# A hybrid attention step on one core: the prompt heads' finish as a job of its own, with a block scratch, and cached loads tied to products

## The chip, the cores and the metric

The kernel runs on one core of a Trainium2 chip. The metric is the device time of one execution in microseconds (us). A core has five engines that run side by side, each through its own list of instructions in order: TensorE (PE, matrix products; PEld is its weight load), VectorE (DVE), ScalarE (ACT), GpSimd (POOL) and SyncE (SP). SP, ACT and POOL also issue DMA transfers; their queues are written SPq, ACTq and POOLq. An instruction that waits holds up all that stand behind it on its engine.

## What is computed

One step of a one-layer streaming encoder: 1024 prompt frames of one stream, and 16 new frames (samples) of each of 8 running streams with 1024 cached frames. Cut to what matters (batch and head reshapes left out):

```python
def reference(x_prompt, x_sample, cache_sb_k, cache_sb_v, state_ret, norm_pre, w_in, sb_head_norm, ret_head_norm, w_out, norm_post):
    # for the prompts, and again for the samples
    h = rms_norm(x, norm_pre)                                 # x: frames x 2048
    q_sb, k_sb, v_sb, gate_sb, q_r, k_r, v_r, gate_r = split(h @ w_in, 8)   # each 8 heads x 128
    q_r, k_r = rope(q_r), rope(k_r) * 128 ** -0.5
    # stick-breaking attention, strictly causal; samples also see the cached keys and values
    z = q_sb @ k_sb.T * 128 ** -0.5
    log_keep = where(strict, log_sigmoid(-z), 0)
    later = reverse_cumsum(log_keep) - log_keep               # over the keys
    o_sb = where(strict, exp(log_sigmoid(z) + later), 0) @ v_sb
    # retention: decayed scores inside a chunk of 64, plus the state carried from chunk to chunk
    o_r, state = retention(q_r, k_r, v_r, log_gamma)
    y = concat(head_rms_norm(o_sb, sb_head_norm) * silu(gate_sb), head_rms_norm(o_r, ret_head_norm) * silu(gate_r))
    return x + rms_norm(y @ w_out, norm_post)                 # and the new k_sb, v_sb, state
```

## The kernel before, in words

All data is float32. Each product of two float32 operands is made as three matmuls of high and low parts (`split` makes them: ACT the high part, DVE the low part; `wh`/`wl` for weights, `mh`/`ml` for the moving rows).

After RMSNorm and transposes the frames are worked in two groups. The first holds prompt tiles 0 to 3 and the sample tile (128 frames each), the second prompt tiles 4 to 7. In each group a loop of `i` from 0 to 7 goes over the heads. "Head 1.2" below is `i` = 2 of the second group (the code counts groups from 0). A head's projections stand in this order: retention q (`q_r`), `k_r`, at even `i` the value rows of two heads (`rows_vr`, `project_rows`), the retention gate, then the stick-breaking q, k, at even `i` the value rows of two heads, and the gate (`gate_sb`). In the second group a projection has 48 matmuls 512 wide, value rows 192 matmuls 256 wide. Samples ride along at even `i` in both groups (`decode`).

The attention work is not written in line. It consists of generators wrapped in `Job`: `tick()`, called after each product, moves on the one job that is due, and a `yield D_...` says how many products later it wants to go on. The constants D_* hold a pair where the two groups differ. `drain(job)` runs a job to its end at once. `place(inst)` binds an instruction behind the last product in the order only: no wait is added. A scheduler with its own costs then sets the final order of each engine.

The names and places that matter:
- `Out.finish`: the head norm of an attention row. DVE scales `so` (prompts, 128x512) by the inverse root mean square; ACTq writes it to a DRAM scratch `s_o` (`turn_out`); `D_TO` products later SPq reads it back in four transfers, turned by blocks (`turn_in`); `D_TI` products later DVE transposes it within blocks into a scratch `oT`, multiplies it with the gain and the gate `sg`, and ACTq writes `s_y`. The retention rows do the same with `ro` and `rg`; the samples' rows with `os` and `gs` (128x128).
- For the prompts' rows that scratch was `kT` (`finish(0, h, rest["sg"], kT, ...)`, line 844). `kT` is the tile into which ACT evacuates the key projection of the next head (line 892), and it has one buffer. On ACT `kh`, the high part of the keys, stands right behind it (L135).
- `sb_job` holds scores, `turn_out`/`turn_in` of the weights, the product with the values (`pa<-vn,kp`, line 588, after the transposition `kp<-be`, line 553) and the finish. The loop drains it after the next head's `q_sb` projection.
- The scores `z<-kh,qh` (own keys) and `z<-kph,qh` (the first group's keys) are line 564.
- `decode` reads cached keys (`kc`, four POOLq transfers each, line 616, three buffers) and cached values (`vc`, SPq, line 654, a pool of three shared with `kcT`); DVE transposes `kc` to `kcT` (line 646), PE multiplies with `vc` in `pd` (line 688).
- The projections have two PSUM banks for each half (`acc0`, `acc1`). A bank comes free once its evacuation is done; that of `gate_sb` goes into `sg`, a tile with one buffer that the head before still holds until its finish has written `s_y`.

After the second group comes the output projection: panels `a3<-wh3,mh` (lines 974 to 976), the first of which also carries the rest of head 1.7's jobs. That stretch, from the end of head 1.7's `gate_sb` to the last drained job, is called the tail below.

Of the kernel before, what the change touches and what calls it, by code (L numbers as in the profile page):

```python
# [36 lines left out]
D_ZP = (2, 2)  # L37
D_AV = (22, 20)
D_ZC = 24
# [5 lines left out]
V_BUFS = 3  # L45
D_RET = (9, 5)
D_TO = (26, 23)
# [11 lines left out]
def tile_hybrid_step(  # L59
# [231 lines left out]
    with ExitStack() as s1:  # L291
# [218 lines left out]
        def acc_tile():  # L510
            return psa.tile([P, 512], F32, name="pa", tag="pa")

        class Out:
# [9 lines left out]
            def finish(self, b, h, gT, oT, dst):  # L523
                rs = inv_rms(op, self.ssq, P, "o")
                nc.vector.tensor_tensor(
                    self.o, self.o, rs.unsqueeze(2).to_broadcast([P, self.nt, P]), ALU.mult
                )
                s = turn_out(self.o, f"s_o{b}_{h}_{self.nt}")
                yield D_TO[phase[0]]
                flat = self.o.rearrange("p k d -> p (k d)")  # L530
                turn_in(s, flat, nc.sync)
                yield D_TI[phase[0]]
                n = self.nt * P
                place(nc.vector.transpose(oT[:, :n], flat))
                nc.vector.scalar_tensor_tensor(
                    gT[:, :n], oT[:, :n], gains[:, b, h : h + 1], gT[:, :n], ALU.mult, ALU.mult
                )
                nc.scalar.dma_start(dst, gT[:, : self.nt * P])

        def z_pieces(n):  # L540
            return [(s, min(512, n - s)) for s in range(0, n, 512)]

        def stick_breaking(tiles, h, out, q2, keys, rest):
            todo = list(enumerate(tiles))
            lag, kinds = 2, ("pcr" if todo[0][1] else ("kp", "be", "cp"))
            rows = []
            for step in range(len(todo) + lag):
# [28 lines left out]
                if step >= lag:  # L576
# [4 lines left out]
                    if step >= len(todo):  # L581
                        yield D_TR[phase[0]]
                    while "vn" not in rest:
                        yield 3
                    vn = rest["vn"]
                    po = acc_tile()
                    for j in range(t + 1):
# [4 lines left out]
                    out.done(i)  # L592
                yield D_AV[phase[0]]

        def decode(h, qs, rest):
# [16 lines left out]
            def load(m):  # L612
                s, j, c = chunk(m)
                kc = dp.tile([P, 512], F32, name="kc", tag="kc", bufs=3)
                for i in range(4):
                    nc.gpsimd.dma_start(  # L616
                        kc[32 * i : 32 * i + 32, :].rearrange("p (k d) -> p k d", d=32),
                        cache_k[0, 2 * c + j, s * 512 : (s + 1) * 512, h, 32 * i : 32 * i + 32].rearrange(
                            "(k p) d -> p k d", p=32
                        ),  # L620
                    )
                return kc
# [28 lines left out]
            def load_v():  # L651
                k = len(values)
                vc = dp.tile([P, NB, P], F32, name="vc", tag="kv", bufs=V_BUFS)
                nc.sync.dma_start(
                    vc, cache_v[0, :, k * P : (k + 1) * P, h, :].rearrange("b p d -> p b d")
                )
                values.append(vc)
# [39 lines left out]
            out.done(0)  # L697
            oT = op.tile([P, P], F32, name="osT", tag="osT", bufs=1)
            ends.append(Job(out.finish(0, h, rest["gs"], oT, s_ys[h]), 2))

# [94 lines left out]
        def ret_branch(gi, g, h, rq, rk, rv, rg):  # L795
# [4 lines left out]
            s = turn_out(rk[:, : nt * P].rearrange("p (k t) -> p k t", t=P), f"s_rk{gi}_{h}")  # L800
            yield D_TO[phase[0]]
            raw = out.o.rearrange("p k d -> p (k d)")
            turn_in(s, raw, nc.sync)
            yield D_TI[phase[0]]
            place(nc.vector.transpose(rkn.rearrange("p k d -> p (k d)")[:, : nt * P], raw))
# [6 lines left out]

        def sb_branch(gi, tiles, h, out, q2, keys, kT, rest, ks):
            off = 4 * gi
# [18 lines left out]
            yield D_NAT[phase[0]]  # L833
            yield from stick_breaking(tiles, h, out, q2, keys, rest)
            vn = rest["vn"]
# [6 lines left out]
            while "sg" not in rest:  # L842
                yield 3
            yield from out.finish(0, h, rest["sg"], kT, s_y[gi][h][:, : 4 * P])

        from_h = lambda k: [(0, NMAX, s_h[:, k, :])]
        from_y = lambda k: [(0, 3 * P, s_y[0][k][:, : 3 * P])]
        ret_job = sb_job = dec_job = loads = None
        ends = []
        for gi, g in enumerate(GROUPS):  # L850
# [7 lines left out]
            for i in range(H):  # L858
# [21 lines left out]
                if sample:  # L880
                    drain(dec_job)
                    while len(ends) > 1:
                        drain(ends.pop(0))
                    qs = kq.tile([P, P], F32, name="qs", tag="qs")
                    nc.scalar.activation(qs, acc[1][0][:, 2 * P : 3 * P], AF.Copy)
                    dec_job = Job(decode(h, qs, rest), D_DEC)
                out = Out(4, "so")
                acc = project(pieces, mov, col(1, h))
# [11 lines left out]
                if gi == 1:  # L900
# [4 lines left out]
                    keys = [old, k2]  # L905
                sb_job = Job(sb_branch(gi, tiles, h, out, q2, keys, kT, rest, ks), D_NAT[phase[0]])
                if i % 2 == 0:
# [16 lines left out]
                if i == H - 1:  # L924
# [3 lines left out]
                    next(loads)  # L928
                acc = project(pieces, mov, col(3, h), loads, (2, 3))
                sg = ep.tile([P, NB_TOK], F32, name="sg", tag="sg")  # L930
                for a, (o, m) in acc:
# [55 lines left out]
        drain(dec_job)  # L987
        for job in ends:
            drain(job)
# [169 lines left out]
```

## Time and profile before

| | |
|---|---|
| median of 3 runs | 2593.51 us (2589.94 to 2596.11) |
| the profiled execution | 2584.93 us, of which the span in the trace is 2583.2 us |
| PE busy | 2398.9 us (93% of the span) |
| DVE busy | 1263.0 us (49%) |
| ACT busy | 932.9 us (36%) |
| POOL busy | 710.3 us (27%) |
| mean granted clock of TensorE | 0.961 of full speed |

PE is the busiest engine by far. So the time is PE's work, at the clock that it is granted, plus the stretches in which PE waits; those are what the order of the other engines' work can move. A row such as `PE z L564 <- ACT kh L135: 60.5, 4, 18.0` in the list of waits says: PE, at line 564, writing tile `z`, waited for ACT's write of `kh` at line 135; 60.5 us in all, 4 times, 18.0 us at the longest. In a timeline the columns are start and duration in us, engine, line and instruction; in brackets stands how long the engine had been idle, and what ended it.

### The profile page before, as it was taken

The page shows a single profiled execution, that of the slowest core. Times are in us where ns is not written, and L with a number is a line of the kernel's source. Part 1 is how long each engine was busy: PE and PEld are TensorE (multiplying, and loading weights), DVE is VectorE, ACT ScalarE, POOL GpSimd, SP SyncE. Part 2 cuts the span into 40 slices and gives each one's busy share as a digit, 9 for nine tenths or more (in the row PEclk, how much of TensorE's full clock was granted, in tenths as well). Part 3 has the DMA queues.
Part 4 walks back from the last instruction along what each step waited for, and adds up shares of the span by engine and source line. Part 5 has one row for each costly group of instructions (what it writes and reads, how often), then busy time and mean ns, then how long its engine had stood idle before and what let it go on. Part 6 is the DMA issues. An engine that isn't in the chain of part 4 may idle for free. (4 is left out here: it accounts for less than half of the span.)

```text
span 2583.2 us, 40506 instructions
## 1 busy us (share of the span) xinstructions
PE 2398.9 (93%) x14832; PEld 2113.2 (82%) x14832; DVE 1263.0 (49%) x2454; ACT 932.9 (36%) x1953; POOL 710.3 (27%) x1133
## 2 busy tenths in 40 slices
PE   7999999999999999899969996999799957999998
PEld 7999899979998998599748975897579745778787
DVE  7245534544455344555544554455544544465544
ACT  6333333323333333343333333333333342344343
POOL 3134214421442144214331433133313322000000
PEclk9999999999999999999989998999899978999999
DMA  7757846684658466866776667666766567576554
GB/s 240 183 131 159 209 106 158 139 205 104 159 138 206 107 162 142 216 170 160 149 149 158 162 147 150 161 159 145 161 157 160 136 165 172 182 225 198 172 177 146
DMA packets 635288, 421.30 MB, mean 163 GB/s; under 512 B 187856, under 2 KB 578000, under 8 KB 632656
## 3 DMA queue, kind: packets, MB, share of 16 engines
q1 hardware_dynamic: 526000, 287.30, 44.3%
q0 software_dynamic: 36608, 80.80, 13.9%
q10 hardware_dynamic: 72480, 50.61, 6.5%
q8 instruction: 116, 1.90, 0.3%
q14 instruction: 84, 0.69, 0.1%
HBM read 337.55 MB, written 81.00 MB: 162 GB/s over the span
## 5 line engine op out<-in xcount | busy, mean ns | idle before, releaser
L136 DVE TENSOR_TENSOR wl<-wr,wh 128x512 fp32r<-128x512 f32 (+1 forms) x576 | 394.4, 690 | 687.9 <-ACT wh L135 676.3
L229 PE MATMUL acc<-mh,wh 128*128 128x512 f32 (+2 forms) x2304 | 665.5, 341 | 5.8 <-ACT mh L135 5.1
L229 PE MATMUL acc<-ml,wh 128*128 128x512 f32 (+2 forms) x2304 | 668.8, 343 | 1.4 <-DVE ml L136 1.3
L229 PE MATMUL acc<-mh,wl 128*128 128x512 f32 (+2 forms) x2304 | 663.5, 340 | 0.0
L135 ACT ACTIVATE wh<-wr 128x512 fp32r<-128x512 f32 (+1 forms) x576 | 356.8, 625 | 840.8 <-PE acc L229 443.9
L616 POOL DMA_DIRECT2D kc<-cache_sb_k x512 | 332.1, 655 | 512.9 <-DVE qp L598 161.1
L229 PEld LDWEIGHTS acc<-mh,wh 128*128 128x128 f32 x2304 | 425.1, 190 | 51.4 <-ACT mh L135 9.5
L229 PEld LDWEIGHTS acc<-ml,wh 128*128 128x128 f32 x2304 | 425.6, 190 | 41.6 <-issue 9.1
L229 PEld LDWEIGHTS acc<-mh,wl 128*128 128x128 f32 x2304 | 425.9, 189 | 38.9 <-issue 9.6
L274 PE MATMUL accn<-whn,mh 128*128 128x256 f32 x1152 | 333.2, 289 | 4.7 <-DVE rk L317 4.6
L274 PE MATMUL accn<-wln,mh 128*128 128x256 f32 x1152 | 325.9, 283 | 0.1
L274 PE MATMUL accn<-whn,ml 128*128 128x256 f32 x1152 | 325.8, 283 | 0.0
L274 PEld LDWEIGHTS accn<-whn,mh 128*128 128x128 f32 x1152 | 220.7, 192 | 21.6 <-issue 11.6
L975 PE MATMUL a<-wl,mh 128*128 128x512 f32 (+1 forms) x576 | 222.7, 387 | 8.5 <-DVE wl L136 8.5
L974 PE MATMUL a<-wh,mh 128*128 128x512 f32 (+1 forms) x576 | 220.3, 385 | 3.8 <-ACT wh L135 3.3
L274 PEld LDWEIGHTS accn<-wln,mh 128*128 128x128 f32 x1152 | 220.9, 192 | 1.1 <-DVE wln L136 0.4
L976 PE MATMUL a<-wh,ml 128*128 128x512 f32 (+1 forms) x576 | 221.3, 384 | 0.0
L274 PEld LDWEIGHTS accn<-whn,ml 128*128 128x128 f32 x1152 | 220.8, 192 | 0.0
L136 DVE TENSOR_TENSOR wln<-wrn,whn 128x512 fp32r<-128x512 f32 x128 | 87.9, 687 | 159.2 <-ACT whn L135 159.0
L135 ACT ACTIVATE whn<-wrn 128x512 fp32r<-128x512 f32 x128 | 81.0, 632 | 212.0 <-PE acc L229 94.0
L975 PEld LDWEIGHTS a<-wl,mh 128*128 128x128 f32 x576 | 109.8, 191 | 32.9 <-DVE wl L136 12.1
L974 PEld LDWEIGHTS a<-wh,mh 128*128 128x128 f32 x576 | 109.9, 191 | 27.0 <-ACT wh L135 4.1
(204 smaller groups left out, 2724.0 us busy)
## 6 DMA issues: line engine op xcount, KB each, us to landing
wr<-w_in SPq DMA_DIRECT2D x384, 256.0 KB, 3.8
wr<-w_out SPq DMA_DIRECT2D x184, 256.0 KB, 3.6
wrn<-w_in SPq DMA_DIRECT2D x128, 256.0 KB, 3.6
kc<-cache_sb_k POOLq DMA_DIRECT2D x512, 64.0 KB, 4.3
vc<-cache_sb_v SPq DMA_DIRECT2D x64, 512.0 KB, 8.1
xt<-x_prompt SPq DMA_DIRECT2D x8, 1024.0 KB, 6.3
xr<-x_prompt SPq DMA_DIRECT2D x8, 1024.0 KB, 6.3
out<-out ACTq DMA_DIRECT2D x12, 512.0 KB, 2.9
```

The source lines that it names most:

```text
L135: nc.scalar.activation(hi, src, AF.Copy)
L136: nc.vector.tensor_tensor(lo, src, hi.bitcast(F32), ALU.subtract)
L229: last = nc.tensor.matmul(a[:, :m], lhs[:, j, :], rhs[w][:, j, o : o + m], start=(w == 0 and j == 0 and n == 0), stop=(w == KT // WQ - 1 a ...
L274: product[0] = nc.tensor.matmul(a, lhs[q][:, jj, ts], rhs[:, j, :], start=(w == 0 and j == 0 and n == 0 and t % 2 == 0), stop=(w == KT // ...
L616: nc.gpsimd.dma_start(kc[32 * i : 32 * i + 32, :].rearrange("p (k d) -> p k d", d=32), cache_k[0, 2 * c + j, s * 512 : (s + 1) * 512, h, 3 ...
L974: nc.tensor.matmul(a[:, :width], hi[q][:, j, ts], wh, start=(k == 0), stop=False)
L975: nc.tensor.matmul(a[:, :width], hi[q][:, j, ts], wl, start=False, stop=False)
L976: product[0] = nc.tensor.matmul(a[:, :width], lo[q][:, j, ts], wh, start=False, stop=(k == KT - 1))
```

## The change

The prompts' finish is no longer part of `sb_job`. `sb_branch` ends by creating a job `ends["p"]`, which the loop drains after the next head's gate projection, before a new `sg` is taken. It no longer uses `kT`: it takes four blocks of 128x128 in turn into one small scratch `oT`, so that each prompt row now costs four transpositions and four multiplications where it had one of each. (The samples' finish, in `ends["d"]`, uses the same scratch in place of its own `osT`.) The tile `so` is created only when the finish before it is done. The loads of `kc` and `vc` are wrapped in `place`, which ties them behind the last product. Three lags change: `D_AV` of the second group from 20 to 16 products, `D_RET` of the first from 9 to 7, and the turn of the retention keys gets its own pair `D_RO`, `D_RI` (21, 23 and 19, 26 for 26, 23 and 24, 26).

```diff
@@ -35,7 +35,7 @@
...
 D_ZP = (2, 2)
-D_AV = (22, 20)
+D_AV = (22, 16)
 D_ZC = 24
...
@@ -43,7 +43,9 @@
...
 V_BUFS = 3
-D_RET = (9, 5)
+D_RET = (7, 5)
+D_RO = (21, 23)
+D_RI = (19, 26)
 D_TO = (26, 23)
...
@@ -531,16 +533,26 @@
...
                 n = self.nt * P
-                place(nc.vector.transpose(oT[:, :n], flat))
-                nc.vector.scalar_tensor_tensor(
-                    gT[:, :n], oT[:, :n], gains[:, b, h : h + 1], gT[:, :n], ALU.mult, ALU.mult
-                )
-                nc.scalar.dma_start(dst, gT[:, : self.nt * P])
+                if oT is not None:
+                    place(nc.vector.transpose(oT[:, :n], flat))
+                    nc.vector.scalar_tensor_tensor(
+                        gT[:, :n], oT[:, :n], gains[:, b, h : h + 1], gT[:, :n], ALU.mult, ALU.mult
+                    )
+                else:
+                    for i in range(self.nt):
+                        c = slice(i * P, (i + 1) * P)
+                        blk = op.tile([P, P], F32, name="oT", tag="oT", bufs=1)
+                        place(nc.vector.transpose(blk, flat[:, c]))
+                        nc.vector.scalar_tensor_tensor(
+                            gT[:, c], blk, gains[:, b, h : h + 1], gT[:, c], ALU.mult, ALU.mult
+                        )
+                nc.scalar.dma_start(dst, gT[:, :n])
 
...
 
-        def stick_breaking(tiles, h, out, q2, keys, rest):
+        def stick_breaking(tiles, h, q2, keys, rest):
+            out = None
             todo = list(enumerate(tiles))
...
@@ -580,9 +592,10 @@
...
                         yield D_TR[phase[0]]
-                    while "vn" not in rest:
+                    while "vn" not in rest or ends["p"] is not None and not ends["p"].done:
                         yield 3
                     vn = rest["vn"]
+                    out = out or Out(4, "so")
                     po = acc_tile()
...
@@ -591,6 +604,9 @@
...
                 yield D_AV[phase[0]]
+            return out
+
+        ends = {"p": None, "d": []}
 
...
@@ -613,12 +629,12 @@
...
                 for i in range(4):
-                    nc.gpsimd.dma_start(
+                    place(nc.gpsimd.dma_start(
                         kc[32 * i : 32 * i + 32, :].rearrange("p (k d) -> p k d", d=32),
...
                         ),
-                    )
+                    ))
                 return kc
...
@@ -651,9 +667,9 @@
...
                 vc = dp.tile([P, NB, P], F32, name="vc", tag="kv", bufs=V_BUFS)
-                nc.sync.dma_start(
+                place(nc.sync.dma_start(
                     vc, cache_v[0, :, k * P : (k + 1) * P, h, :].rearrange("b p d -> p b d")
-                )
+                ))
                 values.append(vc)
...
@@ -695,8 +711,7 @@
...
             out.done(0)
-            oT = op.tile([P, P], F32, name="osT", tag="osT", bufs=1)
-            ends.append(Job(out.finish(0, h, rest["gs"], oT, s_ys[h]), 2))
+            ends["d"].append(Job(out.finish(0, h, rest["gs"], None, s_ys[h]), 2))
 
...
@@ -798,10 +813,10 @@
...
             s = turn_out(rk[:, : nt * P].rearrange("p (k t) -> p k t", t=P), f"s_rk{gi}_{h}")
-            yield D_TO[phase[0]]
+            yield D_RO[phase[0]]
             raw = out.o.rearrange("p k d -> p (k d)")
             turn_in(s, raw, nc.sync)
-            yield D_TI[phase[0]]
+            yield D_RI[phase[0]]
             place(nc.vector.transpose(rkn.rearrange("p k d -> p (k d)")[:, : nt * P], raw))
...
@@ -810,7 +825,7 @@
...
 
-        def sb_branch(gi, tiles, h, out, q2, keys, kT, rest, ks):
+        def sb_branch(gi, tiles, h, q2, keys, kT, rest, ks):
             off = 4 * gi
...
@@ -831,7 +846,7 @@
...
             yield D_NAT[phase[0]]
-            yield from stick_breaking(tiles, h, out, q2, keys, rest)
+            out = yield from stick_breaking(tiles, h, q2, keys, rest)
             vn = rest["vn"]
...
@@ -841,12 +856,11 @@
...
                 yield 3
-            yield from out.finish(0, h, rest["sg"], kT, s_y[gi][h][:, : 4 * P])
+            ends["p"] = Job(out.finish(0, h, rest["sg"], None, s_y[gi][h][:, : 4 * P]), 2)
 
...
         ret_job = sb_job = dec_job = loads = None
-        ends = []
         for gi, g in enumerate(GROUPS):
...
@@ -879,12 +893,11 @@
...
                     drain(dec_job)
-                    while len(ends) > 1:
-                        drain(ends.pop(0))
+                    while len(ends["d"]) > 1:
+                        drain(ends["d"].pop(0))
                     qs = kq.tile([P, P], F32, name="qs", tag="qs")
...
                     dec_job = Job(decode(h, qs, rest), D_DEC)
-                out = Out(4, "so")
                 acc = project(pieces, mov, col(1, h))
...
@@ -903,7 +916,7 @@
...
                     keys = [old, k2]
-                sb_job = Job(sb_branch(gi, tiles, h, out, q2, keys, kT, rest, ks), D_NAT[phase[0]])
+                sb_job = Job(sb_branch(gi, tiles, h, q2, keys, kT, rest, ks), D_NAT[phase[0]])
                 if i % 2 == 0:
...
@@ -927,6 +940,7 @@
...
                 acc = project(pieces, mov, col(3, h), loads, (2, 3))
+                drain(ends["p"])
                 sg = ep.tile([P, NB_TOK], F32, name="sg", tag="sg")
...
@@ -985,7 +999,7 @@
...
         drain(dec_job)
-        for job in ends:
+        for job in [ends["p"], *ends["d"]]:
             drain(job)
...
```

The counts on PE, ACT, POOL and SP do not change. DVE has 96 instructions more: 64 + 64 of 128x128 where there were 16 + 16 of 128x512.

Where the instructions go, first on PE at the border from head 1.1 to 1.2. `acc_14125` before and `acc_14195` after is the bank of head 1.2's `q_r`; `pa<-vn,kp` x8 is the last row tile of head 1.0; `z<-kh,qh` the first score of head 1.1 with its own keys. Before:

```order
L662 MATMUL zn<-ks,qs 128x128
L726 MATMUL pa<-rv,sc 128x128
L731 MATMUL pa<-S,rq 128x128
L564 MATMUL z<-kh,qh 128x256
L564 MATMUL z<-kph,qh 128x512
L564 MATMUL z<-kpl,qh 128x512
L564 MATMUL z<-kl,qh 128x256
L564 MATMUL z<-kh,ql 128x256
L229 MATMUL acc_14125<-mh_11587,wh 128x512
L229 MATMUL acc_14125<-ml_11588,wh 128x512
```

After:

```order
L231 MATMUL acc_14195<-mh_11827,wl 128x512
L601 MATMUL pa<-vn,kp 128x128 x8
L741 MATMUL pa<-rv,sc 128x128
L746 MATMUL pa<-S,rq 128x128
L756 MATMUL pS<-rv,rkn 128x128
L741 MATMUL pa<-rv,sc 128x128
L746 MATMUL pa<-S,rq 128x128
L756 MATMUL pS<-rv,rkn 128x128
L576 MATMUL z<-kph,qh 128x512
L576 MATMUL z<-kpl,qh 128x512
L576 MATMUL z<-kph,ql 128x512
L576 MATMUL z<-kh,qh 128x256
```

Before, the 48 products of `q_r` of head 1.2 start behind `z<-kh,qh`. After, all 48 stand ahead of `pa<-vn,kp`, and `z<-kh,qh` comes some rows after it.

ACT at the same border. `kT<-acc_13914` (before) and `kT<-acc_13880` (after) are the key evacuation of head 1.1, `s_y_1_136<-sg` the write that ends the finish of head 1.0. Before:

```order
L144 ACTIVATE or<-ov 128x4
L465 DMA s_o_0_4_13903<-ro 128x4x128
L538 DMA s_y_1_136<-sg 128x512
L892 ACTIVATE kT<-acc_13914 128x512
L135 ACTIVATE kh<-acc_13914 128x512
L301 ACT_TABLE_LOAD
L301 ACTIVATE sg<-acc_14013 128x512
L490 ACTIVATE kp<-z 128x128
```

After:

```order
L137 ACTIVATE qh<-acc_13759 128x512
L137 ACTIVATE wh<-wr 128x512 x4
L905 ACTIVATE kT<-acc_13880 128x512
L137 ACTIVATE kh<-acc_13880 128x512
L523 ACTIVATE sq,ssq_13521<-so 128x128
L137 ACTIVATE wh<-wr 128x512 x8
L316 ACTIVATE sw<-acc_14195 64x512
L317 ACTIVATE sw<-acc_14195 64x512
L523 ACTIVATE sq,ssq_13521<-so 128x128
L749 ACTIVATE ro<-pa 128x128
```

Before, `kT` and `kh` stand behind the finish of head 1.0; after, they stand right behind the projection, ahead of eight weight splits (four of `gate_sb`, four of the next `q_r`), and the finish is further down.

DVE where the finish of head 1.0 ends. `acc_14013` and `acc_14066` are the bank of head 1.1's gate projection. Before:

```order
L534 STREAM_TRANSPOSE kT<-so 128x512
L535 SCALAR_TENSOR_TENSOR sg<-kT,gains,sg 128x512
L817 STREAM_TRANSPOSE kn<-kT 128x512
L136 TENSOR_TENSOR kl<-acc_13914,kh 128x512
L302 TENSOR_TENSOR sg<-sg,acc_14013 128x512
L534 STREAM_TRANSPOSE rk<-ro 128x512
```

After:

```order
L546 SCALAR_TENSOR_TENSOR sg<-oT,gains,sg 128x128
L510 TENSOR_TENSOR be<-be,kp 128x768
L545 STREAM_TRANSPOSE oT<-so 128x128
L546 SCALAR_TENSOR_TENSOR sg<-oT,gains,sg 128x128
L545 STREAM_TRANSPOSE oT<-so 128x128
L546 SCALAR_TENSOR_TENSOR sg<-oT,gains,sg 128x128
L138 TENSOR_TENSOR wln<-wrn,whn 128x512
L545 STREAM_TRANSPOSE oT<-so 128x128
L546 SCALAR_TENSOR_TENSOR sg<-oT,gains,sg 128x128
L318 TENSOR_TENSOR sw<-sw,sinT 128x512
L138 TENSOR_TENSOR wln<-wrn,whn 128x512
L304 TENSOR_TENSOR sg<-sg,acc_14066 128x512
```

Before, the finish is two instructions. After, it is eight (the first transposition and the piece of the scan L509 stand just ahead of these rows), with a scan and its product (L509, L510), a weight split (`wln`) and a rope product (L318) between them, and the gate's last instruction, which frees its bank, comes three rows behind it.

## The prediction

> **What bounds the kernel now.** I read the engines' busy times first, then the span cut by stage, then PE's list of waits, then the timeline around its longest wait.
>
> ```profile
> PE 2398.9 (93%) x14832; PEld 2113.2 (82%) x14832; DVE 1263.0 (49%) x2454; ACT 932.9 (36%) x1953; POOL 710.3 (27%) x1133
> ```
>
> The change adds no work to PE, so only the 7% in which PE waits and the stretches at a low clock can be won. Cut by stage (us, then PE's busy time, and further right PEclk, the granted clock): group 1, group 2, the tail, the output projection.
>
> ```profile
> 305.00:1070.00 765.00, 748.93 (x5214) 688.26 (x5212) 363.92 (x787) 262.53 (x568) 247.90 (x415) 0.99 0.63 153
> 1070.00:2082.00 1012.00, 922.62 (x5535) 795.34 (x5536) 497.08 (x891) 350.97 (x724) 324.89 (x517) 0.95 0.67 157
> 2082.00:2203.00 121.00, 75.59 (x336) 53.49 (x335) 54.17 (x99) 39.78 (x89) 23.86 (x37) 0.73 0.64 154
> 2203.00:2583.00 380.00, 363.44 (x1727) 305.23 (x1725) 194.11 (x341) 154.91 (x333) 16.72 (x7) 0.99 0.58 187
> ```
>
> PE is idle for 16.1 us in group 1, 89.4 in group 2, 45.4 in the tail. So the loss lies in group 2 and the tail. PE's waits name it:
>
> ```profile
> PE z L564 <- ACT kh L135: 60.5, 4, 18.0
> PE pa L588 <- DVE kp L553: 30.8, 10, 9.8
> PE pd L688 <- DMA vc<-cache_sb_v: 23.5, 11, 3.9
> PE z L564 <- DVE st L782: 4.7, 6, 1.8
> PE accn L274 <- DVE rk L317: 4.6, 3, 2.4
> ```
>
> The largest is four waits for `kh`, three at the borders from odd to even heads of group 2 and one in the tail. The timeline of the first:
>
> ```profile
> 1295.40 0.69 DVE L136 TENSOR_TENSOR wl<-wr,wh 128x512 fp32r<-128x512 f32 x1 [2.02 <-ACT wh L135]
> 1296.01 1.24 DVE L553 STREAM_TRANSPOSE kp<-be 128x1024 f32<-128x1024 f32 x1
> 1297.31 3.25 PE L588 MATMUL pa<-vn,kp 128*128 128x128 f32 x16 [2.37 <-DVE kp L553]
> 1305.73 0.40 ACTq L465 DMA_DIRECT2D s_o<-so  x1
> 1315.27 0.37 ACTq L465 DMA_DIRECT2D s_o<-ro  x1
> 1315.96 3.42 SPq L471 DMA_DIRECT2D so<-s_o  x4
> 1319.54 1.31 SPq L471 DMA_DIRECT2D ro<-s_o  x2
> 1323.29 0.71 DVE L534 STREAM_TRANSPOSE kT<-so 128x512 f32<-128x512 f32 x1 [8.05 <-DMA so<-s_o]
> 1324.04 0.75 DVE L535 SCALAR_TENSOR_TENSOR sg<-kT,gains,sg 128x512 f32<-128x512 f32 x1
> 1325.21 0.60 ACT L892 ACTIVATE kT<-acc 128x512 f32<-128x512 f32 x1 [14.18 <-DVE sg L535]
> 1325.70 0.59 ACT L135 ACTIVATE kh<-acc 128x512 fp32r<-128x512 f32 x1
> 1326.34 0.58 PE L564 MATMUL z<-kh,qh 128*128 128x256 f32 x1 [17.97 <-ACT kh L135]
> 1328.23 0.69 DVE L302 TENSOR_TENSOR sg<-sg,acc 128x512 f32<-128x512 f32 x1 [1.11 <-ACT sg L301]
> ```
>
> From the bottom up: PE waits 17.97 us for `kh`; ACT stands 14.18 us in front of `kT` because DVE's finish of the head before still uses `kT`; DVE waits 8.05 us for the finish's read-back. The chain runs from the end of `pa` at 1300.56 to the end of the finish at 1324.79, 24.2 us. During all of it the keys that PE wants lie ready in PSUM.
>
> **The change part by part.**
>
> *The finish without `kT`, drained later.* `kT` and `kh` now stand right behind their projection on ACT, and `q_r` of the next head stands ahead of `pa`. So the `kh` wait goes at three borders: 60.5 less the 11.57 of the tail (its row is below) is 48.9 us, 16.3 each. With it goes a loss of clock. The same stretch cut finer:
>
> ```profile
> 1294.60:1300.60 6.00, 3.58 (x18) 2.96 (x16) 1.85 (x3) 0.63 (x1) 1.29 (x2) 0.78 1.19 174
> 1300.60:1308.40 7.80, 5.88 (x33) 3.65 (x33) 4.37 (x17) 6.70 (x19) 0.41 (x2) 0.95 0.37 75
> 1308.40:1326.40 18.00, 0.06 (x1) 0.06 (x1) 7.80 (x13) 3.76 (x9) 5.56 (x10) 0.59 0.92 191
> 1326.40:1330.40 4.00, 4.00 (x11) 3.29 (x12) 2.03 (x4) 2.23 (x4) 3.13 (x6) 0.50 0.87 150
> 1330.40:1342.00 11.60, 11.60 (x50) 9.51 (x50) 7.02 (x8) 4.00 (x8) 2.08 (x4) 0.93 0.32 99
> 1364.80:1392.10 27.30, 27.30 (x227) 25.90 (x226) 14.25 (x28) 12.81 (x24) 4.58 (x7) 1.00 0.58 158
> ```
>
> After the long wait PE works 4.00 us at clock 0.50: 2.0 us won per border. The 3.58 us at 0.78 behind the wait of 2.37 us (0.8 us lost) stay, because that wait stays. So a wait of 2 to 3 us costs some 0.8 us more than itself, and I charge that below.
>
> [...]
>
> What comes late in its place, per border:
> - `pa` waits for the transposition `kp`. Before, it stood behind one DVE operation of 0.69 (`wl`, 1295.40); now it stands behind the last weight splits of `q_r` and a product of its rope. I take two operations of 0.69, 1.4 us, more (0 to 3). Queued behind it on PE are only the rest of the burst and `k_r`.
> - `k_r` takes the bank that `q_r`'s rope still reads: 0.5 us (0 to 1.4, two operations of 0.69).
> - The finish now ends in the gate's bank. `rows_vr` needs it at its 30th matmul, and the bank is freed by `sg<-sg,acc`, which stands behind the finish. Its chain was 24.2 us from the end of `pa`. The blocks add 1.2 (below); the scan between them, at 2/3 the length of one in the trace, and the weight splits, rope product and gate product some 5 us. That makes 30.4. PE has for it: the burst, 7.8 us; about 2.5 us of scores that now belong to it; 48 products of `k_r` at 0.23 (11.60 us for 50), 11.1; 29 of the 227 matmuls in 27.30 us, 3.5. That makes 24.9, so 5.5 us are missing. But of the chain, 10.2 us went between the writing of `s_o<-so` and its read-back, where that of `ro` took 4.3 (1315.27 to 1319.54); with that figure nothing is missing. Bounds 0 and 5.5; I take 3, the middle, plus 0.8 for the clock.
>
> Queued behind the finish's wait on DVE are weight splits of `rows_vr`; that is the same wait for PE, not a second one. On SPq the read-back stands ahead of weight loads, for at most those same 10.2 us; the splits' buffers cover it.
>
> Per border 16.3 + 2.0 - 1.4 - 0.5 - 3.8 = 12.6, for three 38 us.
>
> *The block scratch.*
>
> ```profile
> L534 DVE STREAM_TRANSPOSE kT<-so 128x512 f32<-128x512 f32 x16 | 11.3, 706 | 19.9 <-DMA so<-s_o 19.9
> L535 DVE SCALAR_TENSOR_TENSOR sg<-kT,gains,sg 128x512 f32<-128x512 f32 x16 | 11.9, 743 | 0.3
> L534 DVE STREAM_TRANSPOSE osT<-os x8: 302/305/313, 354.8 to 2191.3; 128x128 f32<-128x128 f32 x8
> L535 DVE SCALAR_TENSOR_TENSOR gs<-osT,gains,gs x8: 350/351/353, 355.2 to 2191.7; 128x128 f32<-128x128 f32 x8
> ```
>
> Four blocks cost 4 x (305 + 351) = 2624 ns where one piece cost 706 + 743 = 1449: 1.2 us for each of 16 heads, 19 us of DVE. DVE is busy 49% of the span, so I cost it at nothing beyond the 1.2 us in the chain. If that cover were gone it is 19 us.
>
> [...]
>
> *The tail.* Two of its waits:
>
> ```profile
> 2125.97 0.58 PE L564 MATMUL z<-kh,qh 128*128 128x256 f32 x1 [11.57 <-ACT kh L135]
> 2193.13 3.36 PE L588 MATMUL pa<-vn,kp 128*128 128x128 f32 x14 [9.79 <-DVE kp L553]
> ```
>
> The first goes, but the third tile of the first output panel then waits for the gate's bank behind the finish. Its chain is some 27 us, and PE has the burst of 7.8 us and 5 us of scores ahead of it: 14 us of wait, 8 with the quick read-back. What is won is that all scores of the last head come before this wait, so that their scans and turns run during it. The other 33.8 us of idle time in the tail (45.4 - 11.57) are mostly waits for such turns. I take half of them as gone, 17 us, less a wait that is 2.4 to 5 us longer: 12 us won (bounds -5 and 25).
>
> *Shorter lags.* `D_RET`, `D_RO`, `D_RI` in group 1 and the later finish spread the scores and cached products of a border over the next head's first products. Of group 1's 16.1 us of idle time I take half: 8 (bounds 0 and 14). `D_AV` in group 2 is in the terms above.
>
> *Cached loads tied to products.*
>
> ```profile
> kc<-cache_sb_k POOLq DMA_DIRECT2D x512, 64.0 KB, 4.3
> vc<-cache_sb_v SPq DMA_DIRECT2D x64, 512.0 KB, 8.1
> L616 POOL DMA_DIRECT2D kc<-cache_sb_k x512 | 332.1, 655 | 512.9 <-DVE qp L598 161.1
> ```
>
> A `kc` needs four issues of 0.655 us and 4.3 to land, 6.9 us; where it is tied late, DVE waits for it, with weight splits behind it, but PE feels that only past the splits that are already done. I take 0. A `vc` lands after 8.1 us; issued only when its slot comes free, it is 20 products ahead of its use, 4.6 us at 0.23, so 3.5 us of wait. That is what the longest waits in the list are (3.9). Eleven of 64 loads wait now; if all 20 later loads of group 2's four sample heads did, it would be 70 us in place of 23.5. Before, most of them do not reach that; I take 5 us more (bounds -10 and 47).
>
> **Sum.** 38 + 12 + 8 - 5 = 53 us. The profiled execution took 2584.93 us, 8.6 less than the median of the runs; against it the forecast is 2532, against the median of 2593.51 it is 2540.
>
> **Rivals.**
> - *The stall only moves to the gate's bank.* For: the finish still takes its 24 us or more from the end of `pa`, and everything behind it needs `sg`. Against: 25 us of PE's work now lie over it. If the finish comes 10 us late at each border, and the tail gains nothing, 3 x (16.3 + 2.0 - 1.9 - 10.8) + 8 - 5 = 20: 2574.
> - *Quick read-back everywhere.* No wait at the gate's bank, the tail at 25, group 1 at 12, loads unchanged: 3 x 16.4 + 37 = 86: 2508.
> - *Slower: the tied loads come late.* The mechanism is `vc` on SPq: each later load of both groups, 5 in each of 8 sample heads, starts too late. From (53 + 5) / 40 = 1.5 us more for each on, the gain is gone; at 3 us for each, 120 - 58 = 62 us slower: 2655. Against it: the three first loads of a head are early either way, and in group 1 a product is two matmuls, 256 and 384 wide, so that 20 of them last longer than 4.6 us.
> - *No change.* DVE's wait for the read-back now stands ahead of the splits of `rows_vr`; if it lasts the whole 16 us beyond their cover, PE waits there as long as before, and the rest cancels out: 2590.
>
> **How the numbers follow.** The forecast (2522 to 2558) has 0.53, the moved stall 0.23, the quick read-back 0.12, no change 0.04, slower 0.08. The range from 2504 to 2576 takes in the first three nearly whole and leaves out the last two. 0.2% (5.2 us) is about what a measurement of this kernel can tell from no change; faster by more is 0.88, within it 0.04, slower 0.08.
>
> **What the changed profile would show.** Right: no row of PE's waits for `kh` over 2 us; idle time in group 2 down from 89 to about 50 and in the tail from 45 to about 33; `accn<-...` waiting 2 to 5 us for DVE's `sg` after `k_r`. Wrong: a wait of 10 us there or at the third tile of the panel; `pd` waiting for `vc` with more than 35 us in all; `wl` or `wln` on PE's list with more than 1 us a time, with DVE waiting for `kc` or `so`.

## The result, and the profile after

The changed kernel takes 2567.14 us (median of 4 runs, 2566.09 to 2569.16) against 2593.31 us before. The ratio is 0.9901 (95% interval 0.9883 to 0.9918): 26 us faster, half of the 53 that were forecast. The two profiled executions differ by only 17.4 us (2584.93 and 2567.49), because that of before was 8.4 us below the median of its runs. The span fell from 2583.2 to 2565.7 us.

The wait that the change aimed at is gone. From the list of PE's waits after the change, the rows that bear on it:

```profile
PE pa L601 <- DVE kp L565: 52.5, 17, 15.4
PE pd L704 <- DMA vc<-cache_sb_v: 22.6, 11, 4.0
PE pd L695 <- DVE kp L690: 10.1, 1, 10.1
PE a L988 <- DVE sg L304: 10.1, 1, 10.1
PE accn L276 <- DVE sg L304: 9.1, 3, 3.6
PE z L576 <- ACT be L493: 7.6, 7, 3.6
```

No row has `z` waiting for `kh` any more (60.5 us before). But `pa` now waits 52.5 us for the row tiles' transposition `kp`, where it waited 30.8. The waits for the gate's bank are there (`sg`, 9.1 us at the three borders and 10.1 at the panel), and at the border of the groups a cached product waits once for 10.1 us.

To see where, I cut both spans at the same points of the work: the end of head 1.0's key projection, the end of head 1.7's gate projection, and the end of the last product of the first three tiles' output. So the rows are all up to and including group 1 and its border (called group 1 below), group 2, and the tail. Columns are length, PE's busy time and, further right, the granted clock. Before:

```profile
0.00:1177.80 1177.80, 1136.39 (x7842) 1042.66 (x7843) 569.12 (x1232) 427.56 (x889) 360.81 (x598) 0.99 0.66 163
1177.80:2082.00 904.20, 823.49 (x4934) 711.86 (x4933) 445.61 (x782) 310.66 (x645) 308.95 (x491) 0.95 0.68 155
2082.00:2301.70 219.70, 173.42 (x766) 134.15 (x765) 104.25 (x200) 83.52 (x192) 23.86 (x37) 0.85 0.65 178
```

After:

```profile
0.00:1167.50 1167.50, 1128.60 (x7836) 1039.00 (x7837) 575.98 (x1271) 428.99 (x885) 360.25 (x597) 0.99 0.65 164
1167.50:2056.50 889.00, 825.05 (x4939) 714.51 (x4938) 451.13 (x825) 309.77 (x650) 315.13 (x487) 0.97 0.73 157
2056.50:2281.50 225.00, 171.99 (x765) 133.08 (x765) 110.40 (x216) 84.72 (x193) 31.06 (x44) 0.86 0.67 177
```

Group 1 is 10.3 us shorter (forecast 8), group 2 15.2 (forecast 38 less some of the loads), and the tail is 5.3 us longer (forecast 12 shorter). The rest of the span is 2.7 us longer.

### The profile page after: what moved, and what is told of

It is laid out like the page before. It is cut to its first block, busy times and chain, and to the rows that moved or that the text cites. A ratio compares the mean times of both kernels' runs of the same rounds, so it can differ in the third digit from the quotient of the medians.

```text
span 2565.7 us, 40640 instructions
## 1 busy us (share of the span) xinstructions
PE 2391.3 (93%) x14832; PEld 2111.3 (82%) x14832; DVE 1281.9 (50%) x2550; ACT 934.9 (36%) x1953; POOL 723.8 (28%) x1133
## 5 line engine op out<-in xcount | busy, mean ns | idle before, releaser
L276 PE MATMUL accn<-whn,mh 128*128 128x256 f32 x1152 | 336.2, 292 | 10.1 <-DVE sg L304 9.1
L276 PEld LDWEIGHTS accn<-whn,mh 128*128 128x128 f32 x1152 | 224.0, 195 | 28.0 <-issue 15.2
L988 PE MATMUL a<-wh,mh 128*128 128x512 f32 (+1 forms) x576 | 222.6, 388 | 13.3 <-DVE sg L304 10.1
L473 POOL DMA_DIRECT2D be<-s_be x128 | 93.7, 737 | 136.6 <-DMA s_be<-be 84.6
```

Of the source, the lines that this page charges most:

```text
L276: product[0] = nc.tensor.matmul(a, lhs[q][:, jj, ts], rhs[:, j, :], start=(w == 0 and j == 0 and n == 0 and t % 2 == 0), stop=(w == KT // ...
L473: place(q.dma_start(raw[32 * i : 32 * i + 32, :].rearrange("p (k a) -> p k a", a=32), s[:, :, 32 * i : 32 * i + 32].rearrange("k (j b) a - ...
L988: nc.tensor.matmul(a[:, :width], hi[q][:, j, ts], wh, start=(k == 0), stop=False)
```

## The first border after the change

The wait that took over is best read in the timeline at the border from head 1.1 to 1.2. POOL, DVE and PE after the change:

```profile
1285.00 0.79 POOL L473 DMA_DIRECT2D be<-s_be  x1 [3.62 <-issue]
1294.60 0.69 DVE L138 TENSOR_TENSOR wl<-wr,wh 128x512 fp32r<-128x512 f32 x1 [2.03 <-ACT wh L137]
1297.32 0.69 DVE L138 TENSOR_TENSOR wl<-wr,wh 128x512 fp32r<-128x512 f32 x1 [2.02 <-ACT wh L137]
1298.54 0.69 DVE L318 TENSOR_TENSOR sw<-sw,sinT 128x512 f32<-128x512 f32 x1 [0.53 <-ACT sw L317]
1299.15 1.24 DVE L565 STREAM_TRANSPOSE kp<-be 128x1024 f32<-128x1024 f32 x1
1300.44 0.82 PE L601 MATMUL pa<-vn,kp 128*128 128x128 f32 x5 [3.59 <-DVE kp L565]
```

The last transfer of the turned weights was issued at 1285.00. DVE idled up to 2 us ahead of each weight split since then, waiting for ACT, and took `kp` only at 1299.15, directly behind the rope product `sw`: the row has no bracket, so it waited for nothing but its place. `sw` needs the end of `q_r`, and with that PE had run out of products. The tail shows the same with another queue ahead, DVE and then PE:

```profile
2077.82 0.56 DVE L138 TENSOR_TENSOR ml<-mr,mh 128x384 fp32r<-128x384 f32 x1 [2.28 <-ACT mh L137]
2078.74 0.56 DVE L138 TENSOR_TENSOR ml<-mr,mh 128x384 fp32r<-128x384 f32 x1 [0.37 <-ACT mh L137]
2081.31 0.56 DVE L138 TENSOR_TENSOR ml<-mr,mh 128x384 fp32r<-128x384 f32 x1 [2.01 <-ACT mh L137]
2081.79 1.24 DVE L565 STREAM_TRANSPOSE kp<-be 128x1024 f32<-128x1024 f32 x1
2083.08 1.22 PE L601 MATMUL pa<-vn,kp 128*128 128x128 f32 x4 [15.37 <-DVE kp L565]
```

Here `kp` stands behind the splits of the panel's moving rows, each of which waits for ACT. Over the whole span DVE waited for no transfer ahead of such a transposition (group of this form, busy, mean ns of one, idle before):

```profile
L565 DVE STREAM_TRANSPOSE kp<-be 128x1024 f32<-128x1024 f32 x8 | 9.9, 1238 | 0.0
```

The transfers themselves were there in time at both places: around the border they landed 4.1 to 5.9 us after their issue, so by about 1291, and in the tail 4.2 to 8.8 us after it, so by about 2065 (last issue at 2056.13). `kp`, which takes 1.24 us, starts 8 and 17 us later, and DVE idled in between. So these two waits are a matter of order on DVE, not of late data; the smaller ones were not followed one by one. Which part of the change made that order, the experiments tell.

## The experiments

All times are medians beside runs of the kernel before on the same chip, whose medians there lay between 2585.8 and 2589.2 us; beside the full change it was 2593.3. So a difference to the full change comes out some 3 to 6 us otherwise by the ratios than by the times, and where that matters both are given. The names in the table are those used below.

| | time, us | ratio to before (95%) |
|---|---|---|
| the full change | 2567.1 | 0.9901 (0.9883 to 0.9918) |
| E1 before, block scratch only | 2562.5 | 0.9905 (0.9885 to 0.9925) |
| E2 finish as a job only | 2576.5 | 0.9951 (0.9932 to 0.9970) |
| E3 full, D_AV 20 | 2565.3 | 0.9922 (0.9903 to 0.9940) |
| E4 full, both loads free | 2539.5 | 0.9817 (0.9795 to 0.9838) |
| E5 full, keys free | 2531.3 | 0.9774 (0.9755 to 0.9792) |
| E6 full, values free | 2569.7 | 0.9933 (0.9918 to 0.9948) |
| E7 full, loads tied in group 1 alone | 2550.4 | 0.9850 (0.9833 to 0.9867) |
| E8 both free, D_AV 20 | 2535.9 | 0.9799 (0.9783 to 0.9815) |
| E9 keys free, D_AV 20 | 2537.5 | 0.9809 (0.9791 to 0.9827) |
| E10 keys free, shorter finish | 2530.1 | 0.9783 (0.9765 to 0.9802) |
| E11 E2 with D_RO, D_RI | 2562.0 | 0.9905 (0.9887 to 0.9922) |
| E12 full, keys tied 24 products earlier | 2554.4 | 0.9866 (0.9844 to 0.9888) |

**E1.** The kernel before, its finish still inside `sb_job`:

```diff
-            yield from out.finish(0, h, rest["sg"], kT, s_y[gi][h][:, : 4 * P])
+            yield from out.finish(0, h, rest["sg"], None, s_y[gi][h][:, : 4 * P])   # four blocks in a 128x128 scratch
```

> The kernel before with one edit: the prompts' finish stays inside sb_job, but takes its four 128x128 blocks into a small scratch instead of kT. Theory A (kT as scratch was the whole of the 18 us wait, and what is left over after it is the time of the row tiles' own turns through DRAM): the four waits of z for kh, 60.5 us, are gone, and the time falls by 20 to 30 us, as in the full change; waits of pa for kp grow from 30.8 to about 45 us. Rival B (the finish as a job of its own is what lets ACT go past it): the waits for kh stay over 40 us and the time changes by less than 5 us.

2562.5 us: this one edit brings as much as the whole change. Two rows of its list of waits:

```profile
PE pa L598 <- DVE kp L563: 20.0, 9, 6.8
PE accn L274 <- DVE sg L302: 14.8, 3, 6.5
```

The wait for `kh` is gone, so it was the scratch alone and not the place of the finish in the program; rival B falls. With it group 1 is about as long as before, 1181.0 us against 1177.8, and group 2 is 27.6 us shorter:

```profile
0.00:1181.00 1181.00, 1139.08 (x7842) 1044.67 (x7843) 576.48 (x1280) 427.83 (x889) 359.96 (x598) 0.98 0.66 162
1181.00:2057.60 876.60, 821.92 (x4933) 712.72 (x4932) 447.53 (x820) 309.50 (x648) 319.25 (x491) 0.97 0.72 160
```

But `pa`'s waits went down, not up to 45: that part of theory A, that the turns through DRAM set what is left, falls too.

**E2.** The full change with the lags of before and both loads free:

```diff
-D_AV = (22, 16)
-D_RET = (7, 5)
-D_RO = (21, 23)
-D_RI = (19, 26)
+D_AV = (22, 20)
+D_RET = (9, 5)
+D_RO = (26, 23)
+D_RI = (24, 26)
...
-                    place(nc.gpsimd.dma_start(
+                    nc.gpsimd.dma_start(
...
-                place(nc.sync.dma_start(
+                nc.sync.dma_start(
```

> The change without its lags and without the tied loads: only the finish as its own job with the block scratch. Theory A: nearly the whole gain of the change, 20 to 30 us below the kernel before; the waits of pa for kp lower than the 52.5 us of the full change, about 40, since the lag D_AV is back at 20 products. Rival C (the tied loads and the shorter lags carry the gain of group 1, about 9 us): 10 to 18 us below the kernel before, the nine missing in group 1.

2576.5 us, within rival C's range, and as C said the loss is in group 1, but it is a loss against before and not a gain that is missing. The same three stretches:

```profile
0.00:1207.20 1207.20, 1145.67 (x7840) 1054.58 (x7841) 577.09 (x1271) 422.18 (x881) 355.46 (x598) 0.98 0.67 159
1207.20:2075.20 868.00, 816.32 (x4935) 709.45 (x4935) 453.05 (x830) 310.86 (x651) 319.41 (x491) 0.97 0.73 162
2075.20:2290.10 214.90, 174.57 (x766) 135.35 (x765) 107.15 (x210) 82.47 (x190) 24.73 (x37) 0.86 0.65 180
```

Group 2 is 36.2 us shorter than before, which is the saving that I had worked out for the borders (38). But group 1 is 29.4 us longer, and that I had not foreseen at all. E1 has the same scratch and doesn't show it, so it comes from the finish as a job of its own, with the lags of before. All of its waits of `accn` for `rk` (15.2 us, 3 times, 4.6 before) and `pS` for `kb` (10.2 us, 4 times, not in the list of before) lie there:

```profile
PE accn L276 <- DVE rk L319: 15.2, 3, 5.2
PE pS L756 <- ACT kb L493: 10.2, 4, 4.3
```

**E3.** The full change with `D_AV = (22, 20)`.

> The full change with D_AV of group 2 back at 20 products. Theory D (the shorter lag brings pa ahead of its turned weights: pa's waits for kp rose from 30.8 to 52.5 us): these waits fall to about 40 us and the time is 5 to 12 us below that of the full change, so about 2557. Rival A (the turn through DRAM takes its time whatever the lag; what pa does not wait for, a later product waits for): within 4 us of the full change, about 2567, with the same sum of PE's waits.

2565.3 us: rival A's number. The waits of `pa` fell to 39.3 us as theory D said, without gain; other waits grew, `pd` for `kp` from 10.1 to 15.3 us and `acc` for `wh` from 2.0 to 11.7.

**E4.** The full change without the two `place` around the loads of `kc` and `vc` (the last two edits of E2's diff).

> The full change with the loads of cached keys and values not tied to products. Theory C (tying them spreads the DMA load and the cached products, which gave the 9 us in group 1): 5 to 12 us slower than the full change, in group 1. Rival E (the tied loads cost: they wait for their place and then collide with the turns): 3 to 10 us faster, with pd's waits for vc under 15 us instead of 22.6. If neither, within 3 us.

2539.5 us, 28 us faster than the full change (22 by the ratios) and far beyond what rival E had allowed. But the reason that E gave is wrong: `pd`'s waits for `vc` are 20.5 us, hardly less than 22.6. What fell is `pa`'s waits for `kp`, from 52.5 to 6.6.

**E5 and E6.** One `place` each taken away, E5 that of the keys, E6 that of the values.

> The full change with only the cached keys' loads free again (cached values stay tied). Theory F (tying the keys is what cost the 28 us between the full change at 2567 and the kernel with both loads free at 2539, because the keys' loads share POOL's queue with the row tiles' turns and their transpositions share DVE's with kp): within 5 us of 2539, pa's waits for kp under 15 us. Rival G (tying the values costs, through SPq): within 5 us of 2567, with pa's waits above 40 us.

> The full change with only the cached values' loads free again (cached keys stay tied). Theory F: within 5 us of the full change, about 2567, pa's waits for kp about 50 us, the tail's still 45 us idle. Rival G: within 5 us of 2539.

E5 takes 2531.3 us, 36 less than the full change (33 by the ratios) and 8 less than theory F's number; E6 2569.7, 3 more than the full change (8 by the ratios, whose intervals just touch). The tied keys' loads carry the whole loss. With the keys free, tying the values is 8 us faster (E5 against E4). E5's border, DVE and PE:

```profile
1283.67 0.69 DVE L138 TENSOR_TENSOR wl<-wr,wh 128x512 fp32r<-128x512 f32 x1 [2.02 <-ACT wh L137]
1284.28 1.24 DVE L565 STREAM_TRANSPOSE kp<-be 128x1024 f32<-128x1024 f32 x1
1285.99 1.95 PE L601 MATMUL pa<-vn,kp 128*128 128x128 f32 x16
1286.39 0.69 DVE L138 TENSOR_TENSOR wl<-wr,wh 128x512 fp32r<-128x512 f32 x1 [0.87 <-ACT wh L137]
```

`kp` now stands between two weight splits of `q_r`, `pa` follows in the middle of `q_r` with no bracket, and PE has products to put between the small steps behind it. The place of `kp` is only the last link: the whole chain of the row tile stands earlier in E5, whose last transfer of these weights is issued at 1264.59, against 1285.00 in the full change. Its three stretches:

```profile
0.00:1163.00 1163.00, 1126.77 (x7836) 1040.22 (x7837) 575.57 (x1271) 430.08 (x885) 361.75 (x598) 0.99 0.66 165
1163.00:2032.10 869.10, 821.27 (x4939) 708.11 (x4939) 449.81 (x829) 311.54 (x652) 319.13 (x491) 0.97 0.72 161
2032.10:2242.80 210.70, 171.82 (x766) 133.91 (x765) 107.47 (x209) 80.80 (x186) 25.88 (x37) 0.87 0.67 184
```

Against before, group 1 is 14.8 us shorter, group 2 35.1 and the tail 9.0.

**E7.** `place` of the cached loads only while `phase[0]` is 0.

> The full change with the cached loads tied in group 1 alone. In the profiles tying gained some 8 us in the first four sample heads' stretches of group 1 and lost 27 us from the border of the groups on. If the two add up: 2539 - 8 = 2531, the fastest so far. If the gain in group 1 was only pushed to the border: 2539 as with both loads free.

2550.4 us: neither. The first heads of group 1 keep their gain, but the stretch from head 0.7's key evacuation to head 1.0's, with the border of the groups, takes 150 us where E4 takes 137.5. The two effects did not add up.

**E8.** E4 with `D_AV = (22, 20)`.

> Both cached loads free, and D_AV of group 2 back at 20 products: what is left of the change is the finish with the block scratch and the shorter lags of retention. Theory H (the lags of retention alone repair what the finish alone lost in group 1, 27 us in the profile; D_AV is worth little): 2540 to 2548, group 1 no longer than before. Rival D' (D_AV at 16 is what makes the rows' products come early enough once the loads are free): above 2550.

2535.9 us, 4 below theory H's range; group 1, at 1166.4 us in the same cut, is no longer than before, as H said. Beside E2 it differs in `D_RET`, `D_RO` and `D_RI` alone: these lags are worth 40 us.

**E9.** E5 with `D_AV = (22, 20)`.

> Keys' loads free, values' loads tied, D_AV of group 2 at 20. With both loads free, 20 was 3.6 us faster than 16 (2535.9 against 2539.5), and tying the values alone was 8 us faster. If the two add up: about 2527. If they gain the same time (waits of pd and pa in group 2): 2531 as with 16.

2537.5 us, 6 slower than with 16, where E8 was 4 faster than E4. A miss on both sides; the best `D_AV` depends on which loads are tied. Beside E8 it ties the values, and is 2 us slower: that tying them gains is so only with 16. The keys cost in all three pairs that differ in them alone: 36 us (33 by the ratios) from E5 to the full change, 30 from E4 to E6, 28 (29) from E9 to E3.

**E10.** E5, the prompts' finish in group 2 with lags of its own:

```diff
+D_PO = (26, 12)
+D_PI = (24, 14)
-                yield D_TO[phase[0]]
+                yield lags[0][phase[0]]
-                yield D_TI[phase[0]]
+                yield lags[1][phase[0]]
```

> Keys' loads free, and the prompts' finish in group 2 with lags of 12 and 14 products in place of 23 and 26, so that its transposition stands some 23 products (5 us) earlier. Theory K (the gate's bank is freed late because the finish is placed late; the 13.3 us wait at the third tile of the first panel and the 1 to 3 us at the borders are its placing): the panel's wait falls to 8 to 9 us, the time to 2526. Rival L (the finish is bound by its transfers, and DVE then waits for them ahead of weight splits): the panel's wait stays within 2 us of 13.3, and the time is 2531 or up to 5 us more.

```profile
PE a L990 <- DVE sg L306: 13.1, 1, 13.1
```

13.1 us instead of 13.3, and the time is unchanged (2530.1 against 2531.3): rival L's numbers. But theory K was not put to the test, because the shorter lags did not move the finish: at the panel its first transposition starts 17.9 us after the writing of `s_o` was issued, against 17.5 in E5. Nor does E5 show DVE waiting for a transfer ahead of it, as L had it: ahead of the finish's 64 transpositions it idled 0.6 us in all. What the trace of E5 does show of this wait is its end: ACT takes the gate out of its bank 5 us after the finish's last write was issued, and waits for that write to land, because `sg` has one buffer.

```profile
2074.45 0.34 ACTq L549 DMA_DIRECT2D s_y<-sg  x1
2079.45 0.60 ACT L303 ACTIVATE sg<-acc 128x512 f32<-128x512 f32 x1 [9.09 <-DMA s_y<-sg]
```

**E11.** E2 with `D_RO = (21, 23)` and `D_RI = (19, 26)`.

> The finish alone (2576) with the two lags of the retention keys' turn, D_RO and D_RI, but D_RET of group 1 still at 9 and D_AV at 20. All lags of retention together were worth 40 us (2576 to 2536). Theory M (the turn of the retention keys comes too late once the finish no longer holds up the order, so that products pS and accn wait): 2540 to 2550. Rival N (the steps of retention, D_RET, carry it): above 2565.

2562.0 us, between M and N. Of the 40 us the turn's lags bring 14 when they come first, and `D_RET` 26 on top of them. The waits of `accn` for `rk` are still 12.8 us.

**E12.** The full change, the keys' loads tied behind the product 24 places back:

```diff
-                    ))
+                    ), 24)    # place(inst, back): behind past[-1 - back]
```

> The full change, but the cached keys' loads are tied behind the product 24 places before, so each may be issued some 5 us earlier; DVE's transposition of the row tile at the border still stands behind all weight splits of the next q_r, and pa behind 47 of its 48 products (25 with the keys free). Theory O (the cost is the order: where kp stands on DVE and pa on PE): within 8 us of the full change, 2559 to 2570, with pa's waits above 35 us. Rival P (the cost is the loads' lead: keys that come late hold up DVE): half of the 36 us or more comes back, 2531 to 2550.

2554.4 us, between the two again; `pa`'s waits fell to 23.0 us. The expectation had the order at the border wrong. On PE `pa` still follows the last products of `q_r`, but on DVE `kp` has moved two places up, ahead of the last weight split and the rope product, and the wait of 3.6 us is gone, here and at the other two borders:

```profile
PE pa L605 <- DVE kp L569: 23.0, 9, 8.5
1291.20 0.69 DVE L138 TENSOR_TENSOR wl<-wr,wh 128x512 fp32r<-128x512 f32 x1 [2.03 <-ACT wh L137]
1291.81 1.24 DVE L569 STREAM_TRANSPOSE kp<-be 128x1024 f32<-128x1024 f32 x1
1293.28 1.95 PE L605 MATMUL pa<-vn,kp 128*128 128x128 f32 x16
1293.91 0.69 DVE L138 TENSOR_TENSOR wl<-wr,wh 128x512 fp32r<-128x512 f32 x1 [0.87 <-ACT wh L137]
1295.13 0.69 DVE L322 TENSOR_TENSOR sw<-sw,sinT 128x512 f32<-128x512 f32 x1 [0.53 <-ACT sw L321]
```

In the tail the wait of 15.37 us is one of 8.5. Cut as above, the tail is 8.5 us shorter than in the full change, group 2 4.9 and group 1 3.2. That is less than `pa`'s waits fell by (29.5 us), since others grew, `pd` for `vc` from 22.6 to 29.4 and `a` for `sg` from 10.1 to 13.6. Since the earlier binding changed both the loads' lead and the order of the other work, the time alone can't tell O from P. But keys that come late do not hold up DVE in the full change: its list has no wait for a `kc`, and its transpositions of the keys stand behind 0.1 us of idle time in all:

```profile
L662 DVE STREAM_TRANSPOSE kcT<-kc 128x512 f32<-128x512 f32 x128 | 89.8, 701 | 0.1
PE zc L652 <- DVE kcT L662: 5.3, 4, 1.5
```

PE's wait for those transpositions rose from 0.7 to 5.3 us, which is the most that late keys can have cost PE directly.

## Why the prediction was right or wrong

- *The `kh` wait goes at three borders, 16.3 us each, and what comes late costs 3 to 4 of it back.* Right as a mechanism, shown alone in E1, and right in size in two kernels with the keys free: group 2 is 36.2 us shorter in E2 and 35.1 in E5, for 38 forecast. The waits at the gate's bank that were forecast with 3 us each are there, 9.1 us for three; in E2 they are 17.5, in E5 0.7.
- *`pa` 1.4 us later.* It waits 3.59 us at the first border instead of 2.37. But some 80 us behind each border the full change has another of 4.1 to 4.7 us, and there the term was missed.
- *The block scratch at nothing.* DVE's busy time rose from 1263.0 to 1281.9 us, the 19 that were worked out, and E1, which has it, is 25 us faster than before. That it costs nothing at all is not shown.
- *The tail, 12 us.* In E5 it is 9.0 shorter, with the wait at the panel at 13.3 us for 14 forecast. In the full change it is 5.3 longer, and the 15.37 us for which `pa` waits there for `kp`, behind the panel's splits, where it waits 1.4 in E5, are about the whole difference between the two (14.3).
- *Shorter lags, 8 us.* Group 1 came out at 10.3, but the working was wrong. The finish as a job of its own costs 29.4 us in group 1 (E2), nearly all of it the job and not its scratch (E1: 3.2), and the lags give 40 (E8 against E2). I had read the lags as an addition to a finish that is free in group 1.
- *Cached loads tied.* This is the step that failed: "I take 0" for `kc`. I priced a tied load only as one that lands late (6.9 us on DVE), and as such it does cost next to nothing: DVE waits for none, PE 5.3 us for the transpositions. What it costs is the order of the other work: tying the keys costs 28 to 36 us, in three pairs of runs. The values, which I charged with 5 us, cost nothing that is clear: by the times tying them is from 8 us faster (E5 against E4) to 2 us slower (E9 against E8).

So the missing half of the forecast is one term, the keys at 0. That the other terms come out as a whole is in part luck. The sum with the values tied and the keys at nothing, 53 us, stands against 57 in E5, whose stages miss in both directions (14.8 for 8 in group 1, 35.1 for 38, 9.0 for 12); the sum with no load tied, 58, against 49 in E4. And the 8 us of group 1 are a loss and a gain that I had not seen.

Of the signs, the one of the `kh` row came true. By the cut above PE's idle time in group 2 fell from 80.7 to 64.0 us (47.8 in E5), not by the 39 that were named, and in the tail it rose from 46.3 to 53.0. A wait of 10 us at the third tile of the panel was named as a sign of being wrong; it is there, 10.1 us, but the sum itself had counted 14, so it tells nothing.

The rival closest in time, the stall at the gate's bank (2574), is not what happened: those waits were 3 us each and not 10.

What stays open: by which of its costs the scheduler moves the row tiles' chain, and with it `kp` and `pa`, when only the keys' loads are bound. That the order carries the whole 28 to 36 us is argued from the traces of the first border and the tail; no run moved `kp` alone. E7, E9 and E12 show that the amount can't be worked out from the bound loads alone.

The fastest kernel here is the change with the keys' loads left free: 2531.3 us (E5), or 2530.1 with the shorter finish (E10), which are equal within their spread; both beat the full change by more than 30 us.

## What to carry to other kernels

Here a scratch tile was shared with a tile that the next stage must fill, and the long chain behind the scratch held up work that has nothing to do with it (60.5 us of waits for `kh`); a small scratch of its own (512 bytes per partition) was worth as much as the whole of this change (25.6 us in E1, 26.2 in the full change). An edit that only binds an order, tying the keys' loads, cost 28 to 36 us, and it didn't show as a late transfer (DVE idled 0.1 us ahead of the keys' transpositions): in such a case, look for an instruction that its consumer waits for and that itself starts without a bracket, behind work of another kind. And when several lags and bindings change together, run the change without each of them before judging it: one part of this one gained 40 us on top of the others (E8 against E2), and one lost about 30.

## What the runs showed of the hardware

From the writing of `s_o` before the change 10.2 us passed to its read-back at one place and 4.3 us shortly after, and I had expected that making the finish quicker or earlier would pay. No run shows whether it does: E10's shorter lags left the finish where it was.

I had charged a wait of 2 to 3 us with 0.8 us of clock. The first stretch behind six waits after the change, three of `pa` (3.6 us each) and three at the gate's bank (2.79, 2.71 and 3.64 us), in order of time within each three; the granted clock is the third number from the end:

```profile
1300.44:1306.00 5.56, 4.91 (x24) 4.24 (x25) 1.83 (x7) 1.39 (x4) 0.00 (x0) 0.69 0.37 85
1555.85:1561.40 5.55, 5.16 (x24) 4.32 (x25) 1.84 (x7) 1.66 (x4) 0.00 (x0) 0.62 0.35 89
1811.22:1816.80 5.58, 5.20 (x22) 4.65 (x22) 1.21 (x5) 0.56 (x3) 0.00 (x0) 0.52 0.34 84
1333.01:1336.00 2.99, 2.99 (x25) 2.99 (x26) 0.54 (x1) 0.63 (x1) 0.00 (x0) 1.00 1.25 213
1588.79:1592.50 3.71, 3.71 (x31) 3.71 (x32) 1.26 (x2) 1.11 (x2) 0.61 (x3) 1.00 1.34 191
1845.53:1850.00 4.47, 4.47 (x21) 4.47 (x22) 0.80 (x2) 0.63 (x1) 1.85 (x3) 0.50 1.04 223
```

By these rows each of the four waits of 3.6 us cost an estimated 1.5 to 2.5 us more than itself (busy time at the clock that was missing), and the two of 2.7 and 2.8 us cost nothing more. The burst behind the wait of 2.37 us before the change, reckoned in the same way, cost an estimated 1.3 us (3.25 us busy at 0.59):

```profile
1297.30:1300.60 3.30, 3.25 (x16) 2.96 (x16) 0.01 (x1) 0.00 (x0) 0.75 (x2) 0.59 1.19 167
```

So a flat charge of 0.8 us was too low for five of these seven waits and too high for two, and the length of a wait did not settle what came after it. Over all of group 2 the granted clock still rose from 0.95 to 0.97, with the three waits for `kh` gone.
